# A streaming-encoder layer: more of the convolution's taps per unit of matmul time, the spatial gate's norms one step apart, and four weight pieces split on VectorE

## The chip, the cores and the metric

The kernel runs on one core of one Trainium2 chip, as one launch that reads every input from the chip's memory and writes the output back. The metric is device microseconds of that launch, the median of several runs. All times below are microseconds (us) unless they are marked ns.

## What is computed

One layer of a hybrid encoder on 512 positions of width 1024, all in float32. `xn` is the RMS-normalised input. Four mixers of width 512 read it, each result is projected to 1024 and weighted by its own gate, and the sum goes through an output projection; an MLP with squared ReLU and a gated embedding follow.

```
xn = rms_norm(h); (sg_u, sg_v, g_q, g_k, g_v, g_r, g_a, a_q, a_k, a_v, c_a, c_g) = split(xn @ w_in)
y_a = gelu(sg_u) * (W_s @ layer_norm(gelu(sg_v)) + b_s)          # spatial gate: per block of 128, 4 channel groups
y_b = gated linear attention                                     # state recurrence over chunks of 64
y_c = chunked attention with a relative bias                     # 8 heads
y_d = silu(layer_norm(causal depthwise conv31(c_a * sigmoid(c_g))))
merged = sum_n sigmoid(xn @ w_gate[n] + b_gate[n]) * (y_n @ w_branch[n])
h += merged @ w_out;  h += relu(rms_norm(h) @ w_ff1)^2 @ w_ff2;  h += sigmoid(rms_norm(h) @ W_g + b) * (p @ W_p);  out = rms_norm(h)
```

## The kernel before

**Tiling.** Activations are tiles of 128 channels x 512 positions (or 128 positions x 512 channels). The weights come in pieces of 128 x 1024 numbers. Each float32 product is made of three fast matmuls: a weight piece and an activation are each split into a high part (rounded by ScalarE, `copy` at L231) and a low part (the rest, by VectorE, `tt` at L218), and high x high, high x low and low x high are summed in one PSUM bank of eight. `split_piece` makes the two parts `wh` and `wl` of a piece, up to three pieces ahead of their use. For the pieces in the set `BY_DMA` the low part is made otherwise: ScalarE writes the negated high part into `wl`, and GpSimd issues a DMA that adds the weights onto it (L308).

**Order.** The order is written out by the Python program: it goes through *steps* (`step`), and a step is some 24 matmuls (a gate or projection tile of 5.4 us, or a product of the block scheme, 2.9 us). At the start of a step (`advance`), generators on the list `side` are moved on by one `yield` each; in its middle they get a second chance, and `prefetch` splits further pieces; after the matmuls `fill` runs, and then the step's evacuation `evac`. Every engine works through its own queue in that order, so what stands ahead in a queue has to be done first.

**The convolution.** Its 31 taps on 4 channel tiles, 124 VectorE instructions on 128 x 512 (`taps`; in the trace `u<-pad,vecs,u`, L222), are the *filler*: `fill` issues taps while the VectorE time booked since the convolution's inputs were ready is below `FILL` times the TensorE time booked. `mm` books n / 2.4 ns for a matmul of n columns. When the last tap is out, `conv_norm` joins the side list: sums over channels, a matmul with `mean`, subtraction, squares, `token_stats`, `power` on GpSimd, `spread` (four transposes), and then for each of the four channel tiles a chain that goes to and fro between VectorE and ScalarE: multiply, scale and shift, tanh (L854), combine, round, and subtract for the low part. That chain has a `yield` behind the second and the fourth tile. The result `yd` is needed by the branch products of mixer 3, whose gate steps come last: `branch_product` calls `wait_for`, which moves the side list on until `yd` is there.

**The spatial gate.** The four tiles of `gelu(sg_v)` are normalised by `sg_norm`: BN_STATS and BN_AGGR and a small addition on VectorE, `power` on GpSimd, then (one step later) a subtract-and-scale on VectorE and two additions or multiplications on GpSimd (L1019, L1020). Four steps make `sg_u` (two of them stand between the first products of the gate scheme). Then `sg_mix` runs in two halves, in two successive steps: 16 small matmuls, and per channel group two additions or multiplications and a split, again to and fro between VectorE and ScalarE.

**The gate scheme.** For the gates of mixers 1, 0 and 3, `gate_steps` gives the order Q5 B2 Q1 B3 Q6 Q2 Q7 Q3 Q4 B0 B1 for each of six pairs (mixer, half). A Q is a product with a combined operand (24 matmuls of 256 columns), a B a branch product (12 matmuls of 512 columns). B2 and B3 belong to the pair before. In the first pair the `sg_u` steps stand where B2 and B3 would be. Q1, Q6, Q7 and Q4 share one bank: Q6 has to wait until Q1's value is copied out, and Q4 until VectorE has subtracted Q7's value (`gb<-gb,b`). A bank comes round again eight allocations later.

Of the kernel before, what the change touches and what calls it, by code (L numbers as in the profile page):

```python
# [7 lines left out]
F32R = mybir.dt.float32r  # L8
# [15 lines left out]
COL = {}  # L24
# [14 lines left out]
W_SLOTS = 5  # L39
LEAD = 3  # L40
RAW = 4
FILL = 0.72
WARM = 4
E_SLOTS = 28
PAD = 8
# [35 lines left out]
def layout():  # L81
# [79 lines left out]
    for half in range(2):  # L161
# [5 lines left out]
PIECES, LOADS = layout()  # L167

BY_DMA = {j for j, (srcs, n, onto) in enumerate(LOADS) if PIECES[srcs[0]][0] in ("gate", "br") and PIECES[srcs[0]][1] == 2
          or PIECES[srcs[0]][1:3] in (("w_in", COL["sg_v"]),) + tuple(("w_in", COL["sg_u"] + 128 * m) for m in range(4))}  # L170
GROWN = {e[2] for e in LOADS if e[2] is not None}


def build(tc, x, w, vec, wa2, sgw, rows, rb, pt, out):
# [11 lines left out]
    cost = {"pe": 0.0, "dve": 0.0}  # L186
# [5 lines left out]
    def U(dt=F32):  # L192
        return epool.tile([128, 512], dt, tag="u", bufs=E_SLOTS, name=name("u"))
# [13 lines left out]
    def small(n):  # L207
        return gpool.tile([128, n], F32, tag=f"s{n}", bufs=8, name=name("s"))

    def size(ap):  # L210
        n = 1
        for d in ap.shape[1:]:
            n *= d
        return n
# [9 lines left out]
    def ts(o, a, s1, s2, op0, op1=None):  # L224
        cost["dve"] += 60 + 0.55 * size(o)
        if op1 is None:
            return DVE.tensor_scalar(o, a, s1, None, op0=op0)
        return DVE.tensor_scalar(o, a, s1, s2, op0=op0, op1=op1)
# [3 lines left out]

    def mm(o, l, r, start, stop, **k):
        n = max(size(r), 256)
        cost["pe"] += n / 2.4 * (1 if r.dtype == F32R else 4)
        PE.matmul(o, l, r, start=start, stop=stop, **k)  # L236

    def transpose(o, i):
# [108 lines left out]
    def start(g, wait=0, first=False):  # L347
        side.insert(0 if first else len(side), [g, wait, "start"])

    def fill():  # L350
        while filler and cost["dve"] < FILL * cost["pe"]:
            try:
                next(filler[0])
            except StopIteration:
                filler.pop(0)
# [19 lines left out]
    def tok_steps(key, pieces, xs, nw, after, counts=None, lead=LEAD):  # L375

        bs = [bank() for _ in range(4)]
        k0 = 0
        for i in range(pieces):
            n = counts[i] if counts else 2  # L380

            def mms(_, i=i, n=n, k0=k0):
                for k in range(n):
                    if k == n // 2:
                        middle()
                    for tb in range(4):
                        tok_mm(bs[tb][:, :nw], base[key] + i, k, tb, xs[k0 + k], nw, k0 + k == 0, k0 + k == NKD - 1)

            step(base[key] + i, mms, None, own=False, lead=lead)
            k0 += n  # L390
        for tb in range(4):
            after(tb, bs[tb])


    def ch_mm(b, j, xs, c0=0, width=128):

        hi, lo = parts[j]
        n = len(xs)
        sl = lambda t, k: t[:, k * width + c0:k * width + c0 + 128]
        seq = []  # L400
        for k in range(n - 1):
            seq += [(hi, k, 0), (hi, k, 1)]
        seq += [(lo, k, 0) for k in range(n - 1)]
        seq += [(hi, n - 1, 0), (hi, n - 1, 1), (lo, n - 1, 0)]
        for i, (t, k, q) in enumerate(seq):
            if i == len(seq) // 2:
                middle()
            mm(b, sl(t, k), xs[k][q], i == 0, i == len(seq) - 1)

    def tok_mm(o, j, i, tb, xk, nw, first, last, c0=0, cn=None):  # L410

        hi, lo = parts[j]
        c = slice(i * nw + c0, i * nw + c0 + (cn or nw))
        t = slice(tb * 128, tb * 128 + 128)
        mm(o, xk[0][:, t], hi[:, c], first, False)
        mm(o, xk[0][:, t], lo[:, c], False, False)
        mm(o, xk[1][:, t], hi[:, c], False, last)

    def power(ms, n):
        r = small(n)  # L420
        POOL.tensor_tensor(r, ms, mhalf[:, :n], op=OP.pow)
        return r
# [116 lines left out]
    for tb in range(4):  # L539
        av.append([])  # L540
        for i in range(2):
            t = U(F32R)
# [127 lines left out]
    def after(tb, b):  # L670
        if tb % 2 == 0:
            gk.append(H())
        copy(gk[-1][:, (tb % 2) * 256:(tb % 2) * 256 + 256], b[:, 0:256], scale=r1[:, tb:tb + 1])
        copy(alr[:, tb * 16:tb * 16 + 16], b[:, 256:272], scale=r1[:, tb:tb + 1])

    tok_steps("gka", 3, xg, 272, after, (3, 3, 2))
    start(gla(), 1, True)

# [332 lines left out]
    def sg_norm(tb, t):  # L1011
        bs, ag, sh = small(6), small(2), small(1)
        DVE.bn_stats(bs, t)
        DVE.bn_aggr(ag, bs)
        ts(sh, ag[:, 1:2], EPS, None, OP.add)
        r = power(sh, 1)
        yield
        ts(t, t, ag[:, 0:1], r, OP.subtract, OP.mult)
        POOL.tensor_tensor(t, t, rowt[0], op=OP.mult)  # L1019
        POOL.tensor_tensor(t, t, rowt[1], op=OP.add)  # L1020
# [15 lines left out]
    def after(tb, b):  # L1036
        t = U()
        ACT.activation(t, b, AF.Gelu_apprx_tanh)
        vn.append(t)
        start(sg_norm(tb, t), 0)  # L1040

    tok_steps("sg_v", 4, xn, 512, after)
    def sg_u(m, j):
# [337 lines left out]
    for g in range(4):  # L1381
        for e in ORDER if g < 3 else ORDER_LAST:
            n = (MAKE if g < 3 else MAKE_LAST).get(e)
            if g == 2 and e == "Q4":
                n = "next s1"
# [203 lines left out]
```

## Time and profile before

| | |
|---|---|
| median of 3 runs | 1010.29 us (1009.96 to 1010.33) |
| the profiled execution: its own time | 1009.05 us |
| its span, first to last instruction | 1007.3 us |
| TensorE busy | 973.5 us, 97% of the span |
| VectorE busy | 688.7 us, 68% |
| ScalarE, GpSimd busy | 461.9 us, 113.8 us |
| granted TensorE clock, mean | 0.987 of full speed |

The profiled execution lies 1.24 us under the median. A view in order of time lists merged instructions: start, duration, what it is, how many (x), and in brackets how long the engine had been idle before and what ended that. A view of the waits names who waited for whom. A view by stretches gives each engine's busy time in a piece of the span, and the clock that TensorE was granted there.

### The profile page before, as it was taken

The numbers are of one execution on the slowest core, as the hardware profiler recorded it, in microseconds if no ns is written. First come the engines' busy times: TensorE is split into PE (matmuls) and PEld (weight loads), VectorE is DVE, ScalarE is ACT, GpSimd is POOL, SyncE is SP. The second block draws the span as 40 slices with busy tenths as digits, with TensorE's granted clock in tenths as the row PEclk, the third lists the DMA queues.
The fourth block names the chain that finished last, engine by engine and source line by source line (L and its number), as shares of the span: only waits on it lengthen the run. The fifth ranks groups of instructions, "written<-read, shape, count | busy, mean of one in ns | idle before, by whom it ended". The sixth has DMA issues, their size and how long they took to land.

```text
span 1007.3 us, 12897 instructions
## 1 busy us (share of the span) xinstructions
PE 973.5 (97%) x4982; PEld 823.9 (82%) x4982; DVE 688.7 (68%) x988; ACT 461.9 (46%) x689; POOL 113.8 (11%) x131
## 2 busy tenths in 40 slices
PE   8999999999999889999869999999999999999995
PEld 6978888887888779999849888888888888887885
DVE  7746896477898976666766653366577577578656
ACT  6564764235454343444434433454244335335643
POOL 5001000012113500111100000001011002011000
PEclk9999999999999999999969999999999999999998
DMA  6434322357598746876624324348268277677402
GB/s 235 128 106 143 98 95 66 102 141 193 111 297 196 171 108 177 219 184 185 208 73 146 106 86 144 84 126 208 99 149 194 75 221 170 203 175 181 145 22 84
DMA packets 43945, 147.31 MB, mean 146 GB/s; under 512 B 4939, under 2 KB 5356, under 8 KB 43884
## 3 DMA queue, kind: packets, MB, share of 16 engines
q1 hardware_dynamic: 32300, 104.55, 30.3%
q0 software_dynamic: 11584, 41.95, 23.0%
q8 instruction: 39, 0.64, 0.3%
q14 instruction: 22, 0.18, 0.1%
HBM read 142.28 MB, written 2.10 MB: 143 GB/s over the span
## 4 chain that ended last, share of the span: by engine, by line
PE 88%; DVE 5%; issue 2%; ACT 2%; POOL 1%; DMA 1%; SPq 0%; POOLq 0%; ACTq 0%; DVEq 0%
PE b L236 86%; PE b L240 2%; DVE wl L218 1%; DVE u L218 1%; DMA wl<-w 1%; DVE ht L218 1%; POOL u L1019 1%; ACT wh L231 1%; POOL u L1020 1%; ACT u L231 0%; DMA raw<-w 0%; DVE s L218 0%; ACT combo L231 0%; DVE u L222 0%; ACT u L854 0%
## 5 line engine op out<-in xcount | busy, mean ns | idle before, releaser
L236 PE MATMUL b<-x,wh 128*128 128x512 f32 (+1 forms) x1440 | 317.1, 365 | 5.1 <-DVE gb L218 4.3
L236 PEld LDWEIGHTS b<-x,wh 128*128 128x128 f32 x1440 | 245.4, 190 | 46.6 <-issue 6.6
L218 DVE TENSOR_TENSOR wl<-raw,wh 128x1024 fp32r<-128x1024 f32 (+2 forms) x146 | 178.4, 1231 | 71.9 <-ACT wh L231 70.8
L231 ACT ACTIVATE wh<-raw 128x1024 fp32r<-128x1024 f32 (+2 forms) x166 | 169.9, 1040 | 19.7 <-PE b L236 13.3
L236 PE MATMUL b<-x,wl 128*128 128x512 f32 (+1 forms) x720 | 168.4, 361 | 2.9 <-DMA wl<-w 2.9
L236 PEld LDWEIGHTS b<-x,wl 128*128 128x128 f32 x720 | 124.0, 189 | 24.1 <-DMA wl<-w 3.4
L236 PE MATMUL b<-wh,combo 128*128 128x512 f32 x448 | 141.6, 390 | 0.5 <-DVE ht L218 0.5
L236 PE MATMUL b<-u,wh 128*128 128x512 f32 x320 | 88.8, 406 | 11.2 <-ACT u L231 11.2
L236 PEld LDWEIGHTS b<-wh,combo 128*128 128x128 f32 x448 | 84.1, 188 | 18.3 <-issue 0.9
L236 PE MATMUL b<-wl,combo 128*128 128x512 f32 x224 | 87.5, 391 | 0.9 <-DVE wl L218 0.9
L1209 ACT ACTIVATE act<-act 128x512 f32<-128x512 f32 x32 | 20.1, 632 | 146.8 <-DVE act L222 146.8
L222 DVE SCALAR_TENSOR_TENSOR u<-pad,vecs,u 128x512 f32<-128x512 f32 x120 | 87.2, 780 | 0.0
L236 PEld LDWEIGHTS b<-u,wh 128*128 128x128 f32 x320 | 60.9, 193 | 27.2 <-ACT u L231 13.2
L294 POOL DMA_DIRECT2D grow<-w x42 | 37.6, 953 | 393.5 <-DVE wl L218 300.4
L218 DVE TENSOR_TENSOR wl<-grow,wh 128x1024 fp32r<-128x1024 f32 x48 | 59.0, 1243 | 17.5 <-ACT wh L231 17.5
L236 PE MATMUL b<-wh,x 128*128 128x512 f32 (+1 forms) x208 | 60.8, 374 | 0.0
L222 DVE SCALAR_TENSOR_TENSOR act<-b,v 128x512 f32<-128x512 f32 x32 | 22.0, 690 | 53.6 <-PE b L236 53.3
L236 PE MATMUL b<-wh,u 128*128 128x512 f32 (+1 forms) x192 | 54.4, 367 | 1.1 <-ACT wh L231 1.1
L231 ACT ACTIVATE wh<-grow 128x1024 fp32r<-128x1024 f32 x48 | 49.3, 1049 | 7.7 <-DMA grow<-w 7.5
L236 PEld LDWEIGHTS b<-wl,combo 128*128 128x128 f32 x224 | 42.1, 188 | 10.7 <-DVE wl L218 2.1
L236 PE MATMUL b<-u,wl 128*128 128x512 f32 x160 | 47.6, 396 | 0.0
L236 PEld LDWEIGHTS b<-wh,x 128*128 128x128 f32 x208 | 38.1, 188 | 6.8
(195 smaller groups left out, 1198.0 us busy)
## 6 DMA issues: line engine op xcount, KB each, us to landing
raw<-w SPq DMA_DIRECT2D x161, 512.0 KB, 4.2
grow<-w POOLq DMA_DIRECT2D x42, 512.0 KB, 7.2
wl<-w POOLq DMA_DIRECT2D x20, 512.0 KB, 8.2
grow<-w SPq DMA_DIRECT2D x14, 512.0 KB, 5.7
raw<-w POOLq DMA_DIRECT2D x14, 512.0 KB, 6.2
h<-x SPq DMA_DIRECT2D x16, 256.0 KB, 6.0
v<-rb SPq DMA_DIRECT2D x8, 256.0 KB, 4.1
stack<-stack POOLq DMA_DIRECT2D x8, 256.0 KB, 3.8
```

What stands on the lines that cost most here:

```text
L218: return DVE.tensor_tensor(o, a, b, op=op)
L222: return DVE.scalar_tensor_tensor(o, a, s, b, op0=op0, op1=op1)
L231: return ACT.activation(o, a, AF.Copy, **k)
L236: PE.matmul(o, l, r, start=start, stop=stop, **k)
L240: PE.transpose(o, i, ident)
L294: POOL.dma_start(t[:, 0:n], w[i, :, 0:n], accum_op=OP.add)
L1019: POOL.tensor_tensor(t, t, rowt[0], op=OP.mult)
L1020: POOL.tensor_tensor(t, t, rowt[1], op=OP.add)
L1209: ACT.activation(a, a, AF.Square)
```

## The change

Three edits. `FILL` goes from 0.72 to 0.76, and `mm` books 13 ns more for each matmul, so `fill` issues taps sooner. The four `sg_u` pieces leave the set `BY_DMA`: ScalarE no longer writes the negated copy, GpSimd no longer issues the DMA, and VectorE subtracts. And `sg_norm` of tile `tb` starts `tb` steps later instead of all four at once.

```diff
-FILL = 0.72
+FILL = 0.76
...
-          or PIECES[srcs[0]][1:3] in (("w_in", COL["sg_v"]),) + tuple(("w_in", COL["sg_u"] + 128 * m) for m in range(4))}
+          or PIECES[srcs[0]][1:3] == ("w_in", COL["sg_v"])}
...
-        cost["pe"] += n / 2.4 * (1 if r.dtype == F32R else 4)
+        cost["pe"] += n / 2.4 * (1 if r.dtype == F32R else 4) + 13
...
-        start(sg_norm(tb, t), 0)
+        start(sg_norm(tb, t), tb)
```

The order changes on all engines from the `g_q` steps on. Three places follow.

**VectorE at the spatial gate's norms.** `u` with BN_STATS are the tiles of `sg_v`, `wl` are weight pieces' low parts, `u<-pad,vecs,u` are taps. Before, around the four subtract-and-scales:

```order
L218 TENSOR_TENSOR v_2183<-v_2183,x_585 128x256
L218 TENSOR_TENSOR v_2183<-v_2183,x_587 128x256
L228 TENSOR_SCALAR u_2981<-u_2981,s_2992,s_2997 128x512
L228 TENSOR_SCALAR u_2983<-u_2983,s_3000,s_3005 128x512
L228 TENSOR_SCALAR u_2985<-u_2985,s_3008,s_3013 128x512
L228 TENSOR_SCALAR u_2987<-u_2987,s_3016,s_3021 128x512
L218 TENSOR_TENSOR wl_3089<-raw_2890,wh_3088 128x1024
L222 SCALAR_TENSOR_TENSOR u_1976<-pad_1936,vecs,u_1976 128x512
L222 SCALAR_TENSOR_TENSOR u_1970<-pad_1583,vecs,u_1970 128x512
L222 SCALAR_TENSOR_TENSOR u_1972<-pad_1762,vecs,u_1972 128x512
L222 SCALAR_TENSOR_TENSOR u_1974<-pad_1869,vecs,u_1974 128x512
L218 TENSOR_TENSOR wl_3159<-grow_2780,wh_3158 128x1024
```

And now, from the first of the four on:

```order
L228 TENSOR_SCALAR u_2992<-u_2992,s_3003,s_3008 128x512
L1013 BN_STATS s_3052<-u_2994 128x6
L1014 BN_AGGR s_3053<-s_3052 128x2
L227 TENSOR_SCALAR s_3054<-s_3053 128x1
L218 TENSOR_TENSOR wl_3074<-raw_2904,wh_3073 128x1024
L222 SCALAR_TENSOR_TENSOR u_1970<-pad_1583,vecs,u_1970 128x512
L222 SCALAR_TENSOR_TENSOR u_1972<-pad_1762,vecs,u_1972 128x512
L222 SCALAR_TENSOR_TENSOR u_1974<-pad_1869,vecs,u_1974 128x512
L228 TENSOR_SCALAR u_2994<-u_2994,s_3053,s_3058 128x512
L1013 BN_STATS s_3100<-u_2996 128x6
L1014 BN_AGGR s_3101<-s_3100 128x2
L227 TENSOR_SCALAR s_3102<-s_3101 128x1
```

Before, the four norms stand together, and one low part and four taps follow. Now each norm has a low part and one to four taps behind it. From the linear attention's first reduction (L648) to the first addition of `sg_mix`, VectorE's queue holds 79 taps and 6 low parts before, 88 taps and 10 low parts now; behind `sg_mix` 15 taps are left before and 2 now.

**VectorE at the end of the convolution's norm.** The first tiles named `u` are the chains of the last step of `conv_norm`, four rows for each channel tile; `ga` is a gate tile. Before, the chains of the third and fourth channel tile and what follows:

```order
L218 TENSOR_TENSOR u_4764<-u_1974,u_4736 128x512
L228 TENSOR_SCALAR u_4764<-u_4764,vecs 128x512
L222 SCALAR_TENSOR_TENSOR u_4769<-u_4765,u_4764 128x512
L218 TENSOR_TENSOR u_4772<-u_4769,u_4771 128x512
L218 TENSOR_TENSOR u_4775<-u_1976,u_4736 128x512
L228 TENSOR_SCALAR u_4775<-u_4775,vecs 128x512
L222 SCALAR_TENSOR_TENSOR u_4780<-u_4776,u_4775 128x512
L218 TENSOR_TENSOR u_4783<-u_4780,u_4782 128x512
L218 TENSOR_TENSOR wl_4794<-raw_4601,wh_4793 128x1024
L222 SCALAR_TENSOR_TENSOR ga_4510<-ga_4510,b_4786 128x512
L218 TENSOR_TENSOR u_2295<-u_2295,ga_4510 128x512
L222 SCALAR_TENSOR_TENSOR u_4808<-u_2295,u_4807 128x512
```

And now, from the second channel tile's chain on:

```order
L218 TENSOR_TENSOR u_3803<-u_1972,u_3756 128x512
L228 TENSOR_SCALAR u_3803<-u_3803,vecs 128x512
L222 SCALAR_TENSOR_TENSOR u_3808<-u_3804,u_3803 128x512
L218 TENSOR_TENSOR u_3811<-u_3808,u_3810 128x512
L218 TENSOR_TENSOR wl_3827<-raw_3662,wh_3826 128x1024
L218 TENSOR_TENSOR u_3847<-u_1974,u_3756 128x512
L228 TENSOR_SCALAR u_3847<-u_3847,vecs 128x512
L222 SCALAR_TENSOR_TENSOR u_3852<-u_3848,u_3847 128x512
L218 TENSOR_TENSOR u_3855<-u_3852,u_3854 128x512
L218 TENSOR_TENSOR u_3858<-u_1976,u_3756 128x512
L228 TENSOR_SCALAR u_3858<-u_3858,vecs 128x512
```

Before, nothing stands between the four chains. Now they stand about 60 instructions further ahead in the queue, with a weight piece's low part between the second and the third.

**TensorE at the same place.** The transposes of `spread` (L240), whose result the chains need, and what follows them in TensorE's queue. Before:

```order
L240 MATMUL b_4731<-ident,s_4658 128x128 x4
L236 MATMUL b_4786<-u_4747,wh_4632 128x512
L236 MATMUL b_4786<-u_4748,wh_4632 128x512
L236 MATMUL b_4786<-u_4758,wh_4632 128x512
L236 MATMUL b_4786<-u_4759,wh_4632 128x512
L236 MATMUL b_4786<-u_4771,wh_4632 128x512
```

And now:

```order
L240 MATMUL b_3751<-ident,s_3686 128x128 x4
L236 MATMUL b_3526<-x_423,wh_3658 128x256
L236 MATMUL b_3526<-x_425,wh_3658 128x256
L236 MATMUL b_3526<-x_423,wh_3658 128x256
L236 MATMUL b_3526<-x_425,wh_3658 128x256
L236 MATMUL b_3526<-x_424,wh_3658 128x256
```

Before, the branch product that reads the chains' result (`u` and `wh`) comes right behind the transposes. Now products of the gate scheme follow (Q3 and Q4, then B0, B1, Q5 and so on, which read `x`, `h` and other tiles), and the first branch product that reads `yd` is several hundred matmuls later.

## Rows read from the trace of the kernel before

**Rows 1.** The page: busy time and share of the span by engine

```profile
PE 973.5 (97%) x4982; PEld 823.9 (82%) x4982; DVE 688.7 (68%) x988; ACT 461.9 (46%) x689; POOL 113.8 (11%) x131
```

**Rows 2.** Stretches of the span: us, PE, PEld, DVE, ACT, POOL busy, PEclk, DMA share, GB/s

```profile
318.60:349.40 30.80, 27.86 (x145) 23.69 (x144) 29.62 (x37) 10.89 (x14) 20.08 (x17) 1.00 0.62 144
...
501.00:524.10 23.10, 11.88 (x28) 6.92 (x27) 14.64 (x21) 8.52 (x14) 0.63 (x1) 0.63 0.43 107
```

**Rows 3.** TensorE in order of time around 500 us: start, us, instruction, [idle before it]

```profile
500.67 0.60 PE L240 MATMUL b<-ident,s 128*128 128x128 f32 x4
506.32 1.52 PE L236 MATMUL b<-u,wh 128*128 128x512 f32 x2 [5.06 <-ACT u L231]
...
524.08 2.07 PE L236 MATMUL b<-s,wh 128*128 128x256 f32 x16
```

**Rows 4.** VectorE in order of time, the end of the convolution's norm

```profile
503.67 0.55 DVE L228 TENSOR_SCALAR u<-u,vecs 128x512 f32<-128x512 f32 x1
...
507.63 0.55 DVE L228 TENSOR_SCALAR u<-u,vecs 128x512 f32<-128x512 f32 x1
```

**Rows 5.** ScalarE in order of time, at 500 us

```profile
500.66 1.04 ACT L231 ACTIVATE wh<-raw 128x1024 fp32r<-128x1024 f32 x1
501.61 0.81 ACT L923 ACTIVATE ga<-b,vecs 128x256 f32<-128x256 f32 x2
```

**Rows 6.** TensorE in order of time, 337 to 377 us

```profile
337.85 2.08 PE L236 MATMUL b<-x,wh 128*128 128x256 f32 x16
...
340.72 3.36 PE L236 MATMUL b<-x,wh 128*128 128x512 f32 x14
347.02 1.88 PE L236 MATMUL b<-x,wl 128*128 128x512 f32 x7 [2.94 <-DMA wl<-w]
...
368.99 3.61 PE L236 MATMUL b<-x,wh 128*128 128x256 f32 x16 [4.34 <-DVE gb L218]
...
373.43 1.55 PE L236 MATMUL b<-h,wh 128*128 128x512 f32 x6
...
376.17 1.52 PE L236 MATMUL b<-h,wh 128*128 128x512 f32 x6
```

**Rows 7.** VectorE in order of time, 297 to 369 us

```profile
297.14 0.69 DVE L222 SCALAR_TENSOR_TENSOR u<-u,b 128x512 f32<-128x512 f32 x1 [1.11 <-PE b L236]
...
317.42 0.69 DVE L1013 BATCH_NORM_STATS2 s<-u 128x6 f32<-128x512 f32 x1 [3.59 <-ACT u L1038]
...
318.44 0.68 DVE L1013 BATCH_NORM_STATS2 s<-u 128x6 f32<-128x512 f32 x1
...
321.45 2.73 DVE L222 SCALAR_TENSOR_TENSOR u<-pad,vecs,u 128x512 f32<-128x512 f32 x4
...
324.90 3.86 DVE L228 TENSOR_SCALAR u<-u,s,s 128x512 f32<-128x512 f32 x4
...
330.91 6.89 DVE L222 SCALAR_TENSOR_TENSOR u<-pad,vecs,u 128x512 f32<-128x512 f32 x4
337.72 2.31 DVE L218 TENSOR_TENSOR wl<-grow,wh 128x1024 fp32r<-128x1024 f32 x1
...
345.42 1.23 DVE L218 TENSOR_TENSOR wl<-raw,wh 128x1024 fp32r<-128x1024 f32 x1 [0.94 <-ACT wh L231]
...
350.56 1.43 DVE L218 TENSOR_TENSOR x<-v,x 128x256 fp32r<-128x256 f32 x4 [0.59 <-ACT x L231]
352.42 1.23 DVE L218 TENSOR_TENSOR wl<-raw,wh 128x1024 fp32r<-128x1024 f32 x1 [0.43 <-ACT wh L231]
353.57 0.69 DVE L218 TENSOR_TENSOR u<-b,u 128x512 f32<-128x512 f32 x1
...
368.17 0.68 DVE L218 TENSOR_TENSOR gb<-gb,b 128x512 f32<-128x512 f32 x1
```

**Rows 8.** GpSimd in order of time, the spatial gate's norms

```profile
325.52 1.52 POOL L1019 TENSOR_TENSOR u<-u,u 128x512 f32<-128x512 f32 x1 [2.08 <-DVE u L228]
...
337.32 1.63 POOL L1020 TENSOR_TENSOR u<-u,u 128x512 f32<-128x512 f32 x1
```


## The prediction

> **What bounds the kernel now.** I read the busy shares first: TensorE is busy for 97% of the span [rows 1], so a change can gain only where TensorE waits, and it loses wherever another engine becomes late for it. Then the stretches in which TensorE is not full, and there the order of time.
>
> The largest hole is at 501 us. In the stretch of 23.1 us up to 524.1, TensorE is busy for 11.88 us, at a granted clock of 0.63, a mix of its two levels, 1.2 and 2.4 GHz [rows 2]. The transposes of the convolution's norm end at 501.27, the branch product behind them waits for ScalarE's rounding of the convolution's tiles (5.06 us the first time, and again for each tile), and the next product of the scheme begins at 524.08 [rows 3]. Nothing was put between the transposes and their consumer: taps had been issued so late that the norm's last step fell exactly on the branch that needs it, and `wait_for` emitted it in one piece.
>
> The second hole is at 344 to 373 us. TensorE waits 2.94 us for a low part that a DMA makes, then 4.34 us for VectorE's `gb`, and the product behind the second wait takes 4.44 us (368.99 to 373.43) where the same kind takes 2.87 us at full clock (337.85 to 340.72) [rows 6]. VectorE is busy for 29.62 of 30.80 us there [rows 2], and it runs slowly: while GpSimd multiplies and adds for the norms (325.52 to 338.95) [rows 8], four taps take 6.89 us against 2.73 just before, a low part 2.31 against 1.23 [rows 7]. So this hole belongs to VectorE's queue, and the wait for the DMA inside it is not what ends last: behind it TensorE only reaches `gb` sooner, which VectorE frees at 368.85.
>
> **The change part by part.** *More taps early.* The norm's last step moves from the branch of mixer 3 into the second pair of the gate scheme. What it costs now: two branch products without a wait take 2 x 2.74 us (373.43 to 376.17 is one) [rows 6], so of the 22.8 us from 501.27 to 524.08, 17.3 are lost [rows 3].
>
> What it costs at the new place: one channel tile's chain takes 3.96 us on VectorE (503.67 to 507.63) [rows 4]. Count from the end of Q3's matmuls. VectorE first subtracts `gb`, 0.7 to 0.8 us; two chains end at 8.7; ScalarE is through one subtraction earlier, at 8.0, makes the next piece's high part (1.04 us) and the tanh of Q4's value (0.81 us) [rows 5], at 9.85. TensorE meanwhile does Q4 and two branch products, 2.87 + 5.48 = 8.35 us, and then needs Q4's bank for Q5: it waits 1.5 us. Q5 and B2 last until 15.5. VectorE's low part ends at 10.3 (1.23 us [rows 7]), two more chains put ScalarE through at 17.5, the high part that Q1 needs is there at 18.5: 3.0 us. That is 4.5 us of waiting, and I add 1.6 us for the clock, the 4.44 - 2.87 of the product at 368.99 [rows 6]. 6.1 in place of 17.3 is a gain of 11.2 us. The earlier steps of the norm cost nothing visible now and stay behind products; if a mean or a sum came late there, a step of 2.9 us would be open.
>
> *What the taps displace.* Until the end of the branch of mixer 2, VectorE's queue gets nine taps more since the linear attention's first reduction, 9 x 0.68 = 6.1 us (2.73 / 4 [rows 7]). Its one wait for TensorE there, 1.11 us at 296 [rows 7], takes up a part. I put the delay of the evacuations at nothing for TensorE, since a bank is due again only eight allocations later; ScalarE's copies for the low parts by DMA come later too. Without that cover up to 6 us would show.
>
> *Low parts of `sg_u` on VectorE.* Four subtractions of 1.23 us, 4.9 us, all ahead of `sg_mix`. ScalarE loses four copies, GpSimd four DMA issues; both engines have room, so that gains nothing by itself. The wait of 2.94 us for such a DMA goes, but `gb` is late next, so its time counts only through VectorE.
>
> *The sum at `gb`.* VectorE has 6.1 + 4.9 = 11.0 us more to do before `sg_mix` (88 taps and 10 low parts against 79 and 6 in the order). It has idle time that this fills: 1.11 before 297.14, 3.59 before the statistics, 0.94, 0.59 and 0.43 before `sg_mix` begins at 353.57 [rows 7], 6.7 in all. 4.3 us are left.
>
> *Norms a step apart.* GpSimd's eight operations stay, and so does their cost to VectorE, but other instructions now lie beside them: behind three of the four subtract-and-scales come the next tile's statistics, 1.02 us (317.42 to 318.44) [rows 7]. Whether these slow down beside GpSimd, no row shows. The nearest is the subtract-and-scale: four took 3.86 us as GpSimd began, 0.97 each, where a like one alone takes 0.55 [rows 4, 7]. If the statistics slow down like the taps, the 4.3 us stand; if not at all, 3 x 1.02 us come off, 1.2. I take the middle, 2.8, because the subtract-and-scale slowed less than the taps. The last norm ends later as well, by my count near 349 instead of 338.95 [rows 8], just when the mix's matmuls come up; VectorE is later than they are, so this is covered as long as it stays under about 355. GpSimd's queue has a weight DMA between the norms; it waits for a load that should have landed.
>
> Here the Trainium skill speaks on the open point. "SBUF — State Buffer", section "Who interferes with whom", says that a VectorE instruction with two SBUF inputs contends with a GpSimd instruction that reads SBUF, the second to issue being blocked until the first finishes, and that one with a single SBUF input outside the two-port modes does not contend. The slow taps and low parts agree with it (6.89 against 2.73, 2.31 against 1.23); for the statistics no run here shows it. By that rule the norms' new places would be a gain, and the lower value holds; a plain count of work says 4.3.
>
> The sum: -11.2 + 2.8 = -8.4, from 1009.05 to 1000.65 for an execution like the profiled one. The median of the runs lies 1.24 above it: 1001.9.
>
> **The rivals.** *The statistics run freely beside GpSimd.* They read one tile and write six numbers, which speaks for it; that the subtract-and-scale reads one tile and still slowed speaks against it. Then VectorE is late by 1.2 instead of 2.8, and the median is 1000.3.
>
> *TensorE's clock stays low between the two new waits.* In the old hole it was low beside a wait of 5.06 us and its repetitions, which speaks for it; the new waits are 1.5 and 3.0, and the one of 4.34 us slowed one product only, which speaks against it. If Q5, B2 and Q1 run at half speed, they end at 9.85 + 17.0 = 26.8 instead of 16.8: a loss of 10.0 instead of 6.1, median 1005.8.
>
> *VectorE's queue eats it all: slower.* The place is the stretch from 318 to `gb`. If none of the 6.7 us of idle time is usable (because the waits are round trips that stay), and the GpSimd operations, now spread over about 25 us, shut VectorE out wholly instead of letting it work at 2.73 / 6.89 = 0.4 of its speed for 13.4 us, VectorE is late by 11.0 + 5.3 = 16.3 us: -11.2 + 16.3 gives a median of 1015.4. It decides from a lateness of 11.2 us on. The 29.62 us busy of 30.80 speaks for it, the 3.59 us idle right before against it.
>
> *It does not do what it says: no difference.* If the chains were as exposed at the new place, or VectorE late by 9 to 13 us, the time would stay within 2 us, near 1010. The order speaks against the first: 8.35 us of matmuls that do not need the chains stand behind them, and more behind those.
>
> **How the numbers follow.** My forecast 0.45, the free statistics 0.25, the low clock 0.15, no difference 0.07, slower 0.08. 0.2%, 2 us, is about what a measurement of this kernel can tell from no change. Three of the cases are faster by more than that: 0.85; same 0.07; slower 0.08. The low end: only the second new wait and no clock loss (3.0), and VectorE late by 1.2: -13.1, 997.2. The high end: the low clock together with VectorE late by 4.3: -3.0, 1007.3. What lies beyond is the 0.15 of the last two cases and little else.
>
> **What would show it.** After the change the transposes of the norm should be followed by products, and stand 90 to 100 us earlier, and no wait of TensorE for ScalarE's `u` should be left near 500; behind them two waits of 1 to 3 us, before Q5 and before Q1. TensorE should run without the wait for the DMA at 344, and then wait longer for `gb`, some 8 to 11 us, which ends near 372 instead of 368.85. BN_STATS beside GpSimd's operations should take 0.7 us, or about twice that, and decide the first rival. I am wrong if the wait for `gb` ends past 380, if a wait opens in the branch of mixer 2 (230 to 297), or if the two new waits together reach 10 us.

## The result, and the profile after

The changed kernel takes 998.65 us (median of four runs) against 1010.31 for the kernel before on the same chip: a ratio of 0.9886, 95% interval 0.9852 to 0.9921. The profiled execution's span is 996.8 us, against 1007.3. The profiled pair differs by 10.5 us and the medians by 11.7; the profiled execution of before lay 1.24 us under its median. The gain is 3.3 us more than forecast (1001.9), inside the range. By the 95% interval the gain is 8.0 to 15.0 us, and the 8.4 us of the forecast lie inside it. In the profiled pair 1.55 of the 10.5 us lie ahead of the point where the change reaches TensorE, as shown below; that leaves 8.95.

The busy row of the page and the two stretches that stood in [rows 2] (columns: length; busy us and instructions of TensorE, its weight loads, VectorE, ScalarE, GpSimd; granted clock; DMA share; GB/s), with two that are new holes:

```profile
PE 968.5 (97%) x4982; PEld 823.0 (83%) x4982; DVE 690.9 (69%) x992; ACT 457.7 (46%) x685; POOL 112.3 (11%) x127
```

```profile
318.60:349.40 30.80, 30.80 (x177) 27.14 (x176) 29.89 (x41) 11.82 (x19) 21.05 (x15) 1.00 0.57 139
349.40:372.40 23.00, 14.26 (x110) 14.09 (x109) 17.94 (x27) 7.83 (x13) 0.86 (x1) 0.82 0.34 91
...
400.00:425.00 25.00, 20.44 (x133) 18.64 (x132) 16.55 (x23) 13.43 (x21) 1.77 (x2) 0.94 0.38 85
...
501.00:524.10 23.10, 23.10 (x155) 21.32 (x154) 15.57 (x18) 11.83 (x17) 2.60 (x3) 1.00 0.70 182
```

The old hole at 501 is full, at a clock of 1.00 instead of 0.63. Two holes are left. TensorE in order of time shows them, first behind the mix and then in the pair (1,1) (start, us, instruction, and in brackets the idle time before and what ended it):

```profile
369.35 3.76 PE L236 MATMUL b<-x,wh 128*128 128x256 f32 x16 [8.74 <-DVE gb L218]
...
374.48 1.55 PE L236 MATMUL b<-h,wh 128*128 128x512 f32 x6
...
413.23 2.08 PE L236 MATMUL b<-s,wh 128*128 128x256 f32 x16
...
423.57 3.78 PE L236 MATMUL b<-x,wh 128*128 128x256 f32 x16 [4.56 <-ACT wh L231]
...
428.85 1.57 PE L236 MATMUL b<-h,wh 128*128 128x512 f32 x6
...
434.49 2.08 PE L236 MATMUL b<-x,wh 128*128 128x256 f32 x16
```

The wait for the DMA's low part [rows 6] is gone, and the wait for `gb` grew from 4.34 to 8.74 us, but it ends at 369.35 instead of 368.99. Q5 at 413.23 does not wait; Q1 at 423.57 waits 4.56 us for a weight's high part and then takes 5.28 us (423.57 to 428.85) where a product takes 2.88.

VectorE in the stretch of the norms, which answers to [rows 7]:

```profile
319.23 0.69 DVE L1013 BATCH_NORM_STATS2 s<-u 128x6 f32<-128x512 f32 x1
...
326.57 1.39 DVE L218 TENSOR_TENSOR wl<-raw,wh 128x1024 fp32r<-128x1024 f32 x1
327.88 3.09 DVE L222 SCALAR_TENSOR_TENSOR u<-pad,vecs,u 128x512 f32<-128x512 f32 x3
330.90 0.54 DVE L228 TENSOR_SCALAR u<-u,s,s 128x512 f32<-128x512 f32 x1
331.36 0.68 DVE L1013 BATCH_NORM_STATS2 s<-u 128x6 f32<-128x512 f32 x1
...
338.98 3.77 DVE L222 SCALAR_TENSOR_TENSOR u<-pad,vecs,u 128x512 f32<-128x512 f32 x4
...
368.52 0.68 DVE L218 TENSOR_TENSOR gb<-gb,b 128x512 f32<-128x512 f32 x1
```

The statistics (0.68), three of which run beside a GpSimd operation (325.59, 331.52 and 336.68), keep their undisturbed time; so does the subtract-and-scale (0.54), beside which none of GpSimd's operations on 128 x 512 runs any more. The low parts are less slow than before (1.39 against 2.31). A tap there takes from 0.94 us (four in 3.77) to 1.75 (two in 3.49, at 344.26), against 1.72 before.

**Where the time came from**, by points that both traces have. The two executions are not level when the change reaches TensorE: VectorE reaches the linear attention's first reduction (L648) at 226.41 us, against 227.96 before, and TensorE is equally far on, with the same 1128 matmuls issued. Up to there the change has only put four taps more into VectorE's queue, and it is not what made the difference. In all thirteen profiled executions of this document the point lies between 226.28 and 228.89, with kernels that have the new planner's numbers on either side of the two that have the old ones (227.18 and 227.96). The difference is there after the first 11 us, in TensorE's first products (before, then after):

```profile
7.69 1.05 PE L236 MATMUL b<-wh,u 128*128 128x512 f32 x2
```

```profile
7.56 0.63 PE L236 MATMUL b<-wh,u 128*128 128x512 f32 x2
```

From the reduction to `gb`, before and after:

```profile
227.96:368.17 140.21, 133.75 (x718) 112.94 (x716) 121.31 (x199) 66.15 (x89) 39.32 (x39) 1.00 0.72 179
```

```profile
226.41:368.52 142.11, 134.05 (x718) 112.88 (x716) 129.31 (x211) 62.20 (x85) 38.54 (x35) 0.98 0.64 162
```

VectorE needs 1.90 us more: 8.00 more of work and 6.10 less of idle time. Up to the end of the product behind `gb`, counted from the reduction, the kernel after is 2.60 us later: 1.91 for `gb`, 0.69 because that product is slower (5.13 against 4.44). From there to the end it is 11.55 us faster: the old hole gives 17.3 us, a wait of 0.75 us of TensorE for VectorE that stood at 497.73 in the same norm is gone, and the new place costs 4.56 + 2.40 = 6.96. That makes 11.1; 0.5 us have no place that I can name. The whole is -1.55 + 2.60 - 11.55 = -10.5.

### The profile page after: what moved, and what is told of

Read it like the earlier page. It is cut to its first block, busy times and chain, and to the rows that moved or that the text cites. A ratio compares the mean times of both kernels' runs of the same rounds, so it can differ in the third digit from the quotient of the medians.

```text
span 996.8 us, 12886 instructions
## 1 busy us (share of the span) xinstructions
PE 968.5 (97%) x4982; PEld 823.0 (83%) x4982; DVE 690.9 (69%) x992; ACT 457.7 (46%) x685; POOL 112.3 (11%) x127
## 4 chain that ended last, share of the span: by engine, by line
PE 77%; DVE 12%; issue 4%; DMA 3%; ACT 2%; POOL 1%; SPq 0%; POOLq 0%; ACTq 0%; DVEq 0%
PE b L236 75%; DVE u L222 5%; DVE wl L218 2%; PE b L240 2%; DMA u<-sgw 2%; DVE u L218 1%; DVE ht L218 1%; DVE v L218 1%; DVE s L218 1%; DMA wl<-w 1%; POOL s L421 0%; DMA stack<-stack 0%; ACT wh L231 0%; DMA raw<-w 0%; ACT u L231 0%
## 5 line engine op out<-in xcount | busy, mean ns | idle before, releaser
L218 DVE TENSOR_TENSOR wl<-raw,wh 128x1024 fp32r<-128x1024 f32 (+2 forms) x150 | 182.7, 1226 | 68.1 <-ACT wh L231 66.9
L236 PE MATMUL b<-u,wh 128*128 128x512 f32 x320 | 83.6, 391 | 0.0
```

The lines of the kernel that those rows point to most:

```text
L218: return DVE.tensor_tensor(o, a, b, op=op)
```

## The experiments

The low parts by VectorE were not tried alone. By my count of the order, with the old numbers the taps then end behind the branch that needs them; no run shows it. Two theories stand against each other. **Mine**: the taps moved the convolution's norm to a place where it costs 7 us instead of 17, and VectorE's queue alone sets when `gb` comes, so the other two edits count by what they add to or take from that queue. **The rival**: one of the two other edits earns or spoils the gain by another way, the DMA that makes the low parts above all. Each run has the kernel before beside it, at 1009.4 to 1010.1 us. Between executions whose program is the same so far, the stretch of the norms starts up to 1.6 us apart, so I compare lengths of stretches and not starts. The median of the kernel before differs by up to 0.9 us from one set of runs to another (1009.39 to 1010.31), and a difference between kernels of different sets is no surer than that.

### One edit alone: the norms a step apart

```diff
-        start(sg_norm(tb, t), 0)
+        start(sg_norm(tb, t), tb)
```

> The kernel before with one edit: the gate's norms a step apart. Nothing else moves; the hole at 501 us stays. Theory A (VectorE's queue sets gb, and the stagger cuts what GpSimd costs VectorE): in the trace after the change VectorE lost 5.95 us beside GpSimd where before it lost 8.0, so gb should be freed 2 us earlier, near 367, and the time be 1008.3 (-2.0). Theory B (it only spreads the same loss, or ends so late that the mix waits): 1010 to 1013. Both: TensorE still waits about 2.9 us for the low part by DMA at 344.

Measured: 1005.81, ratio 0.9953 (0.9936 to 0.9970). Theory A had the sign and half of the size, and what both theories took for certain, that the DMA's wait stays, was wrong. GpSimd's queue shows why; the kernel before, then this one:

```profile
337.32 1.63 POOL L1020 TENSOR_TENSOR u<-u,u 128x512 f32<-128x512 f32 x1
338.89 0.87 POOL L294 DMA_DIRECT2D raw<-w  x1
339.47 1.18 POOL L308 DMA_DIRECT2D wl<-w  x1
```

```profile
331.11 1.02 POOL L421 TENSOR_TENSOR s<-s,mhalf 128x1 f32<-128x1 f32 x1
332.09 0.88 POOL L308 DMA_DIRECT2D wl<-w  x1
332.86 1.44 POOL L1019 TENSOR_TENSOR u<-u,u 128x512 f32<-128x512 f32 x1
```

GpSimd issues the DMA for the low part in its turn. In the kernel before, ScalarE's share of it, the negated high part, is ready at 331.25:

```profile
330.20 1.05 ACT L231 ACTIVATE wl<-raw 128x1024 fp32r<-128x1024 f32 x1
```

But the issue stood behind all eight operations of the norms; a step apart, it stands between them, 7.4 us earlier, and TensorE no longer waits 2.94 us. The gain itself is VectorE's, as theory A has it: TensorE still waits for `gb` (4.47 us instead of 4.34), and from the first statistics to `gb` VectorE needs 47.64 us instead of 50.75, with 4.48 us less work (the same instructions, less slowed by GpSimd) and 1.37 more idle time. Theory A had put 2 us for that.

### One edit alone: the taps

```diff
-FILL = 0.72
+FILL = 0.76
...
-        cost["pe"] += n / 2.4 * (1 if r.dtype == F32R else 4)
+        cost["pe"] += n / 2.4 * (1 if r.dtype == F32R else 4) + 13
```

> The kernel before with the planner's numbers alone (0.76 and +13). The low parts stay with the DMA, so the taps come earlier still: the mean's product of the convolution's norm moves to some 4 steps ahead of where it is after the change, right behind the mix. The hole at 501 (17.3 us) goes. Theory A (the chains' cost belongs to the place, about 7 us wherever two chains lie in one step, and is larger while VectorE catches up after the mix): 17.3 goes, 7 to 11 come, gb about 1 us earlier or later: 1000 to 1005. Theory B (all of the gain is this edit's, the two others only pay for it): 998 to 999.

Measured: 1011.19, ratio 1.0009 (0.9996 to 1.0021). Neither theory: the edit with the largest term brings nothing alone. The old hole is gone, and TensorE shows what came instead:

```profile
350.69 3.36 PE L236 MATMUL b<-x,wl 128*128 128x512 f32 x7 [4.66 <-DMA wl<-w]
371.61 1.05 PE L236 MATMUL b<-ones,u 128*128 128x1 f32 x8 [0.47 <-DVE u L218]
379.35 3.46 PE L236 MATMUL b<-x,wh 128*128 128x256 f32 x16 [6.69 <-DVE gb L218]
410.30 3.78 PE L236 MATMUL b<-s,wh 128*128 128x256 f32 x16 [9.37 <-ACT ga L231]
```

With fewer low parts booked on VectorE, the planner issues the last tap earlier still, and the norm's subtractions stand inside the mix, ahead of `gb`. On VectorE:

```profile
366.24 0.68 DVE L218 TENSOR_TENSOR ga<-ga,b 128x512 f32<-128x512 f32 x1
366.83 2.48 DVE L218 TENSOR_TENSOR u<-u,b 128x512 f32<-128x512 f32 x4
```

So I put the norm where the full change has it:

```diff
-        start(conv_norm(), 0)
+        start(conv_norm(), 8)
```

> The kernel before with the planner's numbers (0.76 and +13), and the convolution's norm held back by 8 steps, so that its products stand where they stand after the change; norms all at once, low parts by DMA, as before. Theory A (what the taps alone lost in the run without the hold was the place, right among the mix's steps ahead of gb): the hole at 501 goes for the wait of 4.56 us and the slow product, as after: the gain of 10 us is there, 998 to 1001, with gb freed near 370. Theory B (without the staggered norms the taps cost what they bring): 1005 to 1011.

Measured: 1003.66, ratio 0.9937 (0.9915 to 0.9960), between the two theories. The place accounts for 7.5 us; what is still missing is again the DMA behind GpSimd's norms:

```profile
343.13 1.19 POOL L308 DMA_DIRECT2D wl<-w  x1
```

TensorE waits for it, and VectorE, for once without work, waits for what comes behind that product:

```profile
350.76 3.35 PE L236 MATMUL b<-x,wl 128*128 128x512 f32 x7 [3.65 <-DMA wl<-w]
375.09 3.75 PE L236 MATMUL b<-x,wh 128*128 128x256 f32 x16 [4.17 <-DVE gb L218]
```

```profile
356.36 1.43 DVE L218 TENSOR_TENSOR x<-v,x 128x256 fp32r<-128x256 f32 x4 [5.71 <-ACT x L231]
```

From the first statistics to `gb` VectorE is idle for 10.28 us here and for 4.48 in the kernel after.

### The full change without one edit

The norms all at once again:

```diff
-        start(sg_norm(tb, t), tb)
+        start(sg_norm(tb, t), 0)
```

> The kernel after with one edit undone: the gate's norms all at once again; low parts and taps as after. Theory A (the stagger saved about 2 us of VectorE's time in a queue that sets gb): gb freed near 371 to 372 instead of 369.2, time +2 to +3 us, 1000.7 to 1001.7. Theory B (a norm's place does not matter; the recorded sum held by luck): 998.6 within 0.7.

Measured: 1001.23, ratio 0.9911 (0.9894 to 0.9928), as theory A says. `gb` releases TensorE at 372.06 instead of 369.35; 1.0 us of that lies ahead of the stretch of the norms, which starts at 320.26 instead of 319.23.

The low parts of `sg_u` by DMA again, with the norm at the same place:

```diff
-          or PIECES[srcs[0]][1:3] == ("w_in", COL["sg_v"])}
+          or PIECES[srcs[0]][1:3] in (("w_in", COL["sg_v"]),) + tuple(("w_in", COL["sg_u"] + 128 * m) for m in range(4))}
...
-        start(conv_norm(), 0)
+        start(conv_norm(), 8)
```

> The kernel after with sg_u's low parts by DMA again; the planner then issues two taps more before gb, and the convolution's norm is held back by 8 steps so that its products stand where they stand after the change. VectorE has 4 low parts less (4.9 us) and 2 taps more (1.4 us) ahead of gb, so theory A (VectorE's queue alone sets gb) says gb 3.5 us earlier and 995.2. Theory B (the wait for the DMA's low part, 2.94 us before, counts in full because VectorE is no longer later than it): 998.0 to 999.5. Theory C (taking the low parts from the DMA queue is what earned the gain): 1001 or more.

Measured: 995.86, ratio 0.9857 (0.9842 to 0.9871), theory A. A wait of 1.76 us for the low part of another DMA stands just ahead of the stretch of the norms; in the stretch none comes back, and `gb` is 2.7 us earlier, where theory A had said 3.5:

```profile
314.13 0.50 PE L236 MATMUL b<-wl,x 128*128 128x512 f32 x1 [1.76 <-DMA wl<-w]
366.61 3.15 PE L236 MATMUL b<-x,wh 128*128 128x256 f32 x16 [4.34 <-DVE gb L218]
```

The four versions with the norm of the convolution at the place of the full change:

| median, us | low parts of `sg_u` by DMA | by VectorE |
|---|---|---|
| norms at once | 1003.66 | 1001.23 |
| norms a step apart | 995.86 | 998.65 |

With the norms at once, taking the low parts off the DMA saves 2.4 us; once the norms are a step apart, it costs 2.8. So the two small edits overlap, and the wait for the DMA behind GpSimd's norms, which either of them undoes, is a part of it. From the first statistics to `gb`, with the low parts by DMA, norms at once and then a step apart:

```profile
320.42:374.27 53.85, 46.85 (x279) 41.71 (x277) 43.57 (x59) 22.00 (x32) 20.05 (x17) 0.93 0.50 123
```

```profile
319.49:365.78 46.29, 42.78 (x273) 38.79 (x271) 39.09 (x60) 20.88 (x31) 22.60 (x17) 1.00 0.60 144
```

Of the 7.56 us that the stagger takes off, 4.48 are VectorE's work, on which GpSimd weighs less, and 3.08 its idle time, the DMA's share (the wait of 5.71 us behind the product that needs it is 2.64 now). With the low parts on VectorE the stagger takes off 1.68 (50.97 to 49.29), 2.20 of work against 0.52 more idle time. In the full change the edit of the low parts earns its place through the planner's sums: in the run of the taps alone, which lacks it, the taps carry the norm into the mix. That run has the norms at once; the full change without this edit and without the hold was not run.

### What GpSimd costs VectorE

The two kernels leave out GpSimd's multiplication and addition in the norm, in both orders:

```diff
-        POOL.tensor_tensor(t, t, rowt[0], op=OP.mult)
-        POOL.tensor_tensor(t, t, rowt[1], op=OP.add)
```

> The kernel after without GpSimd's eight operations in the gate's norm (its scale and shift are left out, so the outputs differ): the cost of those operations to VectorE, measured with the norms a step apart. By the summed slow-downs of the trace VectorE loses 5.95 us: gb freed near 363.4 instead of 369.2, and beside nothing the taps take 0.68 and the low parts 1.22 us. If the slow-downs are not GpSimd's, taps and low parts keep their longer times.

> The same left out (scale and shift of the gate's norm), with the norms all at once. Theory A (the stagger's worth is less contention with GpSimd): with no GpSimd work left both orders give the same, gb near 363.4 as without the operations in the staggered order, within 0.7. Theory B (its worth is in VectorE's order and waits): gb 2 to 3 us later here than in the staggered order, as between the two full kernels (372.06 against 369.35).

Measured: 995.85 a step apart and 996.63 at once, of two runs each. From the first statistics to `gb` VectorE needs 44.81 us (320.83 to 365.64) and 44.71 (321.71 to 366.42): without GpSimd's work the order makes no difference, and with it the difference is 49.29 against 50.97. By these lengths theory A holds. The absolute times were 3 to 4 us later than expected, because the stretch started later and VectorE was idle in it for 1.2 us more. VectorE a step apart, without GpSimd's operations:

```profile
328.16 1.23 DVE L218 TENSOR_TENSOR wl<-raw,wh 128x1024 fp32r<-128x1024 f32 x1
329.30 2.07 DVE L222 SCALAR_TENSOR_TENSOR u<-pad,vecs,u 128x512 f32<-128x512 f32 x3
331.29 0.54 DVE L228 TENSOR_SCALAR u<-u,s,s 128x512 f32<-128x512 f32 x1
331.75 0.68 DVE L1013 BATCH_NORM_STATS2 s<-u 128x6 f32<-128x512 f32 x1
```

Against the rows of after: the same three taps 3.09 and 2.07, the same low part 1.39 and 1.23, and the statistics 0.68 in both. Summed from the first statistics to `gb`, eighteen taps take 12.42 us here and 17.58 after, nine low parts 11.05 and 11.70: GpSimd costs 5.8 us after the change. By the same unit times it cost 7.9 before (taps 16.49, seven low parts 10.74, subtract-and-scales 3.86 against 2.16).

### Three changes of the order that start from the kernel after

The first puts the chains of the convolution's norm one to a step:

```diff
             yd.append(split(y))
-            if m % 2:
-                yield
+            yield
```

> The kernel after, with the four chains at the end of the convolution's norm one to a step instead of two. In the trace of after, TensorE waits 4.56 us before Q1 for ScalarE's high part of a weight, which stands behind four chains on VectorE and ScalarE, and Q1 then runs at half speed (5.28 us for 2.88). Theory A (the two chains in a step are the wait): it goes or falls under 1 us, and Q1's clock with it, -5 to -7 us: 991.7 to 993.7. Theory B (the chains' sum is what counts, so the wait only moves to the next product that needs a weight): 997 to 1000, with a wait of 3 to 5 us one to three products later.

Measured: 1000.18, ratio 0.9909 (0.9890 to 0.9928), theory B, 0.2 us over its range. Q1 no longer waits, but Q6 does, for the copy that empties Q1's bank, which stands in ScalarE's queue behind the last chain:

```profile
431.35 3.78 PE L236 MATMUL b<-s,wh 128*128 128x256 f32 x16 [5.44 <-ACT ga L231]
```

```profile
427.35 0.63 ACT L231 ACTIVATE u<-u 128x512 fp32r<-128x512 f32 x1 [0.76 <-DVE u L222]
...
430.73 0.57 ACT L231 ACTIVATE ga<-b 128x512 f32<-128x512 f32 x1
```

What counts is how long the four chains take, not how they are dealt out. In the kernel after, VectorE idles for ScalarE twice in each:

```profile
405.69 0.68 DVE L218 TENSOR_TENSOR u<-u,u 128x512 f32<-128x512 f32 x1
...
407.71 0.69 DVE L222 SCALAR_TENSOR_TENSOR u<-u,u 128x512 f32<-128x512 f32 x1 [0.76 <-ACT u L854]
409.10 1.29 DVE L218 TENSOR_TENSOR u<-u,u 128x512 fp32r<-128x512 f32 x2 [0.70 <-ACT u L231]
```

So the second works on two tiles at a time, stage by stage:

```diff
-        for m in range(4):
-            z, th = U(), U()
-            tt(z, acc[m], rbc, OP.mult)
...
+        for p in (0, 2):
+            zs = [(m, U(), U()) for m in (p, p + 1)]
+            for m, z, th in zs:
+                tt(z, acc[m], rbc, OP.mult)
+                ts(z, z, col("clg", m), col("clb", m), OP.mult, OP.add)
+                ACT.activation(th, z, AF.Tanh)
+            ys = []
+            for m, z, th in zs:
+                y, hi = U(), U(F32R)
+                stt(y, th, 1.0, z, OP.add, OP.mult)
+                copy(hi, y)
+                ys.append((y, hi))
+            for y, hi in ys:
+                lo = U(F32R)
+                tt(lo, y, hi.bitcast(F32), OP.subtract)
+                yd.append((hi, lo))
+            yield
```

> The kernel after, with the chains at the end of the convolution's norm written two tiles at a time, stage by stage (both products, then both halves of tanh, then both roundings, then both low parts). Two to a step as after, the same instructions; VectorE need not idle for ScalarE (0.70 to 0.76 us, twice a chain, 5.8 us of the 17.5 from 405.7 to 423.2). Theory A (the wait is VectorE's and ScalarE's order, the round trips fill it): the high part for Q1 comes near 418, TensorE is not there before 418.9, so the wait of 4.56 us and the 2.4 us of Q1's slow product go, 991.5 to 993. Theory B (as the chains one to a step showed, the wait moves on to the next piece): 996 or more, a wait of 2 us or more left between Q1 and Q6.

Measured: 992.62, ratio 0.9830 (0.9810 to 0.9849), theory A. TensorE has no idle time left in this place (the same stretch as above, 20.44 us busy there):

```profile
400.00:425.00 25.00, 25.00 (x172) 23.30 (x172) 21.21 (x30) 16.29 (x24) 1.80 (x3) 1.00 0.53 142
```

The third does the same with the mix's groups: both sums and products of a pair with their roundings, then both subtractions.

```diff
-        for g in range(4):
...
-            ya.append(split(t))
-            if g % 2:
-                yield
+        for p in (0, 2):
+            ts_ = []
+            for g in (p, p + 1):
...
+                copy(hi, t)
+                ts_.append((t, hi))
+            for t, hi in ts_:
+                lo = U(F32R)
+                tt(lo, t, hi.bitcast(F32), OP.subtract)
+                ya.append((hi, lo))
+            yield
```

> The kernel after, with the gate's mix written two groups at a time (both sums and products, then both roundings, then both low parts), so that VectorE no longer idles for ScalarE's rounding once a group (0.70 to 0.82 us, four times). Same instructions. Theory A (VectorE's queue sets gb): gb freed 2 to 3 us earlier, near 366.5, time 996 to 997. Theory B (something beside VectorE's queue sets gb, the rounding by ScalarE above all): within 0.7 of 998.6.

Measured: 995.00, ratio 0.9856 (0.9841 to 0.9871), theory A, 1 us under its range. In the first pair of groups VectorE idled for ScalarE 0.70 and 0.82 us in the kernel after; now it is 0.16:

```profile
355.85 1.29 DVE L218 TENSOR_TENSOR u<-u,u 128x512 f32<-128x512 f32 x2
357.31 0.69 DVE L218 TENSOR_TENSOR u<-u,u 128x512 fp32r<-128x512 f32 x1 [0.16 <-ACT u L231]
```

and `gb` releases TensorE 3.0 us earlier, at 366.34. The product behind it takes 4.44 us instead of 5.13, which the range had left out.

All that helped, in one kernel (the low parts by DMA, the hold of 8 steps, the mix and the chains two at a time):

> All that helped, together: taps and staggered norms as after, sg_u's low parts by DMA with the convolution's norm held back 8 steps, the mix and the chains two at a time. Alone the low parts by DMA gave -2.8 and the mix -3.65 against after. If gb is set by VectorE's queue all the way, both count: 992.2 with the chains as they were, and with the 6 to 7 us of the chains' wait 985.5 to 987. If the wait for gb ends at TensorE's own arrival or at a DMA first, one of the two is lost: 988 to 990.

Measured: 985.32, ratio 0.9753 (0.9732 to 0.9773), 13 us under the kernel after: every part counts in full, as the three gains alone (2.8, 3.65 and 6.0) add up to 12.5. What is left of the wait for `gb` is 1.45 us, and the product behind it runs at full speed:

```profile
365.46 2.14 PE L236 MATMUL b<-x,wh 128*128 128x256 f32 x16 [1.45 <-DVE gb L218]
...
368.39 1.55 PE L236 MATMUL b<-h,wh 128*128 128x512 f32 x6
```

## Why the prediction was right, and which terms were off

**The old hole (17.3 us).** Right: it is gone, the norm's transposes start at 401.58, 99.1 us earlier than in [rows 3], and no wait for ScalarE's `u` is left.

**The new place (forecast 6.1, measured 6.96).** The sum of the waits was right, 4.5 against 4.56 us, with one of its two parts wrong. I had Q5 wait 1.5 us for Q4's bank; it does not wait at all, since Q5 opens a new bank of the eight. That only moved the time: TensorE reached Q1 earlier by those 1.5 us and waited there for the same high part, counted for 18.5 us after the end of Q3's matmuls and there 18.5 us after it (405.0 to 423.57). The clock's loss was taken from [rows 6] as 1.6; it was 2.4, behind a wait of about the same length. With the 0.75 us of the old wait at 497.73, which I had not counted, the term comes to 11.1 net, against 11.2 forecast. That it is so close is luck in part: 0.8 us too little for the clock and 0.75 us not counted cancel.

**VectorE ahead of `gb` (forecast 2.8, measured 1.9, and 0.69 for the slower product).** Counted from the first reduction, as the forecast was, the mechanism holds and the terms are near. Idle time takes up 6.10 us, where I had 6.7: ahead of the statistics 4.70, just what I had found, and behind them 1.40 instead of 1.96. The work grew by 8.0 us instead of 11.0 less some 1.5; 0.6 of the difference is GpSimd's cost, which fell by more than I took, and 0.9 us have no place that I can name. Two things are not in the forecast: the slower product behind the longer wait, and four taps more ahead of the reduction (30 against 26), 2.7 us of VectorE's work, which idle time there took up. By the times from the start of the profile `gb` comes only 0.36 us later (369.35 against 368.99), but 1.55 us of that comparison is the start of the two executions.

**The statistics beside GpSimd.** I took the middle between free and slow; they run free, 0.68 us, so the first rival's condition is met. The section "Who interferes with whom" of the Trainium skill's page "SBUF — State Buffer" says that a VectorE instruction with one SBUF input, outside the two-port modes, does not contend with GpSimd, and that one with two inputs contends with GpSimd's reads: statistics 0.68 with or without GpSimd's work, three taps 3.09 against 2.07, agree. The subtract-and-scale, which also reads one tile, did slow where it ran beside GpSimd: four took 3.86 us before [rows 7], against 1.91 in the run with the norms at once and without GpSimd's operations:

```profile
330.46 1.91 DVE L228 TENSOR_SCALAR u<-u,s,s 128x512 f32<-128x512 f32 x4
```

Why it differs from the statistics, no run here shows. GpSimd's cost fell by 2.1 us (7.9 to 5.8), where I had put 0 to 3.06.

**The DMA's wait.** I let it go as harmless because `gb` is late behind it. For this change that holds. What I did not see is that the wait came from GpSimd's queue, in which the DMA stood behind the norms: of its place between them I wrote only that its load should have landed. That hides a part of what the second and third edit are worth: the stagger brings 7.8 us where the DMA stays (1003.66 to 995.86), some 3 of them by the DMA's place and the rest by GpSimd's lower cost, and the move to VectorE brings less than nothing beside it. Not the three edits' own prices but their sum came out right.

**The rivals.** The clock did not stay low: Q5 and B2 ran at full speed, and of what follows the wait only Q1 was slow; the Q2 at 434.49 takes 2.88 again. VectorE's queue was never late by 11 us, and no wait opened in the branch of mixer 2 (from 230 to 297 us TensorE is busy for 66.92 of 67.00). The rival "no difference" by an exposed norm was near, though: it is what the taps do alone (1011.19), and by the planner's sums it is the low parts booked on VectorE that keep the full change from it, which no run with the norms a step apart tests.

## What to carry to other kernels

Before pricing a wait for a DMA, look where its issue stands in the issuing engine's queue: here the norms ahead of it on GpSimd made the wait, and moving them cured it for nothing. But look as well what comes next behind the wait: in the run with the norms alone a step apart, TensorE then waited as long for `gb` as before, and the gain came through VectorE. Where two in-order engines pass a tile to and fro, write two tiles stage by stage; dealing the chains out over more steps only moved the wait (1000.18), interleaving them removed it (992.62). And before pricing a stretch from two traces, look whether both executions came to its start at the same time: here 1.55 us of the 10.5 between them lay ahead of the point where the change reaches TensorE.

## What the runs showed of the hardware

**The clock behind a wait.** A product that takes 2.88 us took 5.28 behind a wait of 4.56 us and 5.13 behind 8.74, at granted clocks of 0.50 and 0.52, so nearly all of it at the lower level of 1.2 GHz. Behind 4.34 us in the kernel before it took 4.44 (granted clock 0.62), behind 10.52 us in the run with the norms at once 4.37, and behind 1.45 us 2.93. I had expected the loss to grow with the wait. In these runs it lies between 1.4 and 2.4 us behind all waits for `gb` or at Q1 and Q6 of 4.2 to 10.5 us, without that order, so cutting a wait of 4.34 us to 1.45 gave back the clock's part as well.

**GpSimd's cost depends on what stands beside it.** The same eight operations cost VectorE 7.9 us before, 5.8 after, and 3.6 in the run with the norms alone a step apart, where the first two of them (322.39 to 325.05) fell beside statistics and idle time. Even a tap beside GpSimd is not always doubled: 3.09 for three against 2.07, but 3.49 for two against 1.41.
